# Three of five last-group projections of an SSD mixer moved into its step loop

## The chip, the cores and the metric

The kernel runs on one core of one Trainium2 chip. The metric is the device time of one execution in microseconds (us). The core has five engines with a queue each: TensorE (PE in the profile, its weight loads PEld), VectorE (DVE), ScalarE (ACT), GpSimd (POOL), and SyncE (SP), which here only issues DMAs. An engine works through its own queue in order; a waiting instruction holds up all that stand behind it on that engine.

## The reference, cut to what matters

Two layers of a streaming encoder take 640 tokens of width 1024: 512 of a new stream (four tiles of 128) and 8 x 16 of running streams (a fifth tile). Layer 0 is FFN, mixer, FFN; layer 1 is FFN, Mamba-2 mixer, FFN. Each is wrapped as `x = layer_norm(ALPHA * x + sublayer(x))`. The change is in the second mixer and what surrounds it:

```python
proj = x @ w_in                                   # z | x B C | dt
xbc  = silu(conv(xbc));  dt = softplus(dt_raw + dt_bias)
y, h_last = ssd_recurrence(xs, dt, a, bm, cm, h0)  # 4 groups of 8 heads, state 128
y  = y + d_skip * xs
yg = y * silu(z)                                  # per group of 512 channels
yg = yg * rsqrt(mean(yg ** 2) + RMS_EPS) * norm_g
out = yg @ w_out                                  # 2048 -> 1024
x = layer_norm(ALPHA * x + out)
```

All is in float32. The kernel splits each operand into a high and a low part that TensorE takes at full rate, and adds three products (`mm3`): high x high, low x high, high x low.

## The kernel before, in words

The mixer (`mixer1`) has four groups of heads and five token tiles, so 20 **steps** `(g, c)`, in the order of tiles `ORDER = (4, 0, 1, 2, 3)` in each group: first the tile of the running streams (4), then the new stream's four, whose state is handed on from tile to tile. Steps are counted from 0; steps 15 to 19 are the fourth group's, which the code calls `g == 3`. In the body of step i stand:

- `run_fill(1)`, twice in most steps: one input projection of a later group (`xbc`, `gate_in`) as filler for TensorE. There are 33; the last of them, the fourth group's last gate input, stands at the start of step 16, so steps 17 to 19 have none.
- `core_a` of the next step (loads of B, C, x rows and decays, L1688 to L1712; decay matrix, turned inputs, L1715 to L1739), mostly VectorE and ScalarE work.
- `core_b` of this step (L1747 to L1780: state product on TensorE, the state's decay on POOL at L1763, the sum at L1764, the outputs L1772 to L1779), or `core_s` for tile 4, which reads the running streams' states from tiles named `h0` (four of them, loaded before).
- `gate_out(g - 1, c)`: the out-projection of the group before, one step row later. It loads z rows from DRAM (L1824), multiplies (L1825), squares (L1826), adds up on POOL (L1828, L1829), sums over partitions by a matmul with ones (L1830), makes the RMS factor (L1832, L1833), splits the product into `og`, and runs 24 matmuls (`mm3`, L148) into two banks, which L1841 scales and adds to the residual `yacc`.

After the 20 steps the fourth group's five projections follow, tiles 0 to 4, each with its layer norm (`layer_norm`, L176 to L205: statistics L185 on VectorE, the power L188 on POOL, the scaling L192 on ScalarE, gamma and beta on VectorE L194 and POOL L195 to L197; for the last tile two whole-row VectorE operations, L199 and L205). A norm ends by putting its transposes (L220 to L222: into the channel-major `xhi`, `xlo` that the next matmuls read) on a list, `pend`; `run_pend` emits the oldest of the list. Gamma and beta are loaded by POOL's queue (L173) into `h0` places.

**Buffers.** Weights come by SP's queue into four `raw` tiles and are split (L101 and L102; with a row factor L127 and L128) into the pair tiles `w`, six in all, each of two units. `w1` is a single unit. A group's out-weights are four pair tiles. `ext` and `acc` are row tiles (two each) of the convolution and the gate inputs; `cst` holds the convolution's old rows, which only the `xbc` projections read. The z rows of the fourth group go into `ext` and `acc`, their split results into `og` or `csb`.

**The FFN after it** (`ffn`, ph `ffn3`) starts with two hidden blocks (f = 0, 1) on the first half of the tokens (tiles 0, 1) and then on the second (tiles 2 to 4), 48 matmuls each, with a `run_pend` after each.

**What sets the order.** The program text gives each instruction a rank and its dependences; a planner orders each engine's queue by these and its own estimates of durations, so that an instruction can come out ahead of others that stand before it in the text. `tc.issue_after(x)` keeps what it encloses behind x on x's engine.

## Time and profile before

| | |
|---|---|
| Median of 3 runs | 2508.24 us (2507.06 to 2510.02) |
| The profiled execution's own time | 2512.95 us |
| Its span, first to last instruction | 2511.2 us |
| Granted TensorE clock, mean | 0.999 |
| POOL busy | 382.3 us (15%) |
| DMA rate, mean | 130 GB/s |

How to read the views below: in a table of stretches (times from the span's start) each engine has its busy us and its number of instructions; the last three numbers are the granted clock, the mean busy share of the 16 DMA engines and GB/s. In a list of waits the engine, the tile and the line that waited stand first, then what it waited for, then total us, how often, and the longest. In a group of instructions: line, engine, operation, output and inputs with shapes, count, then busy us and mean ns of one, then the idle time before them. In a timeline: start, us, engine, line, operation, count, and in brackets the idle time before and what ended it.

### The profile page before, as it was taken

The page shows a single profiled execution, that of the slowest core. Times are in us where ns is not written, and L with a number is a line of the kernel's source. Part 1 is how long each engine was busy: PE and PEld are TensorE (multiplying, and loading weights), DVE is VectorE, ACT ScalarE, POOL GpSimd, SP SyncE. Part 2 cuts the span into 40 slices and gives each one's busy share as a digit, 9 for nine tenths or more (in the row PEclk, how much of TensorE's full clock was granted, in tenths as well). Part 3 has the DMA queues.
Part 4 walks back from the last instruction along what each step waited for, and adds up shares of the span by engine and source line. Part 5 has one row for each costly group of instructions (what it writes and reads, how often), then busy time and mean ns, then how long its engine had stood idle before and what let it go on. Part 6 is the DMA issues. An engine that isn't in the chain of part 4 may idle for free. (4 is left out here: it accounts for less than half of the span.)

```text
span 2511.2 us, 40776 instructions
## 1 busy us (share of the span) xinstructions
PE 2475.4 (99%) x15563; PEld 2277.1 (91%) x15563; DVE 2019.0 (80%) x3400; ACT 1285.9 (51%) x2415; POOL 382.3 (15%) x500
## 2 busy tenths in 40 slices
PE   9999999999999999999999999999999999999998
PEld 8999999978789999999999999999999879999897
DVE  7797787666878888878888887787686788898887
ACT  4444454336744555553455554567565543555542
POOL 0000001210130000013000002311111152211121
PEclk9999999999999999999999999999999999999999
DMA  5333344443222433461144434466565623555563
GB/s 187 110 99 99 120 145 138 145 152 114 91 84 68 122 94 106 110 167 58 59 121 111 117 101 133 152 197 189 161 213 149 203 72 102 160 146 168 155 172 113
DMA packets 179092, 326.63 MB, mean 130 GB/s; under 512 B 21408, under 2 KB 91040, under 8 KB 178384
## 3 DMA queue, kind: packets, MB, share of 16 engines
q1 hardware_dynamic: 164032, 293.83, 37.0%
q0 software_dynamic: 14864, 30.19, 6.2%
q8 instruction: 122, 2.00, 0.3%
q14 instruction: 74, 0.61, 0.1%
HBM read 259.56 MB, written 40.54 MB: 120 GB/s over the span
## 5 line engine op out<-in xcount | busy, mean ns | idle before, releaser
L101 ACT CAST w<-raw 128x512 fp32r<-128x512 f32 (+1 forms) x721 | 536.0, 773 | 333.5 <-DVE raw L368 150.9
L102 DVE TENSOR_TENSOR w<-raw,w 128x512 fp32r<-128x512 f32 (+2 forms) x721 | 626.6, 891 | 75.5 <-ACT w L101 73.2
L385 PE MATMUL bank<-xhi,w 128*128 128x320 f32 x2432 | 436.8, 309 | 2.7 <-DVE s L427 1.4
L385 PE MATMUL bank<-T,w 128*128 128x320 f32 x2736 | 430.6, 309 | 3.5 <-ACT bank L402 2.2
L385 PEld LDWEIGHTS bank<-T,w 128*128 128x128 f32 x2736 | 407.1, 188 | 7.3 <-ACT bank L402 5.2
L385 PEld LDWEIGHTS bank<-xhi,w 128*128 128x128 f32 x2432 | 377.2, 188 | 6.7 <-DVE s L427 2.2
L148 PE MATMUL bank<-xhi,w 128*128 128x256 f32 (+2 forms) x2272 | 360.0, 309 | 5.9 <-DVE yacc L1841 1.3
L148 PEld LDWEIGHTS bank<-xhi,w 128*128 128x128 f32 x2272 | 333.5, 187 | 16.1 <-ACT xhi L221 2.4
L148 PE MATMUL bank<-w,h 128*128 128x512 f32 (+1 forms) x1404 | 325.0, 389 | 0.6 <-ACT h L101 0.6
L148 PEld LDWEIGHTS bank<-w,h 128*128 128x128 f32 x1404 | 259.7, 188 | 53.6 <-ACT h L101 2.2
L385 PE MATMUL bank<-xlo,w 128*128 128x320 f32 x1216 | 228.2, 309 | 0.0
L368 DVE TENSOR_TENSOR raw<-raw 128x512 f32<-128x512 f32 x304 | 212.0, 697 | 3.4
L539 POOL DMA_DIRECT2D yacc<-ev x91 | 79.1, 902 | 746.8 <-ACT ev L538 659.6
L385 PEld LDWEIGHTS bank<-xlo,w 128*128 128x128 f32 x1216 | 190.9, 188 | 0.1
L148 PE MATMUL bank<-xlo,w 128*128 128x256 f32 (+2 forms) x1136 | 189.1, 307 | 0.0
L148 PEld LDWEIGHTS bank<-xlo,w 128*128 128x128 f32 x1136 | 170.2, 187 | 0.6
L526 PE MATMUL bank<-w,h 128*128 128x512 f32 x624 | 145.7, 389 | 0.0
L526 PEld LDWEIGHTS bank<-w,h 128*128 128x128 f32 x624 | 116.8, 188 | 24.7 <-DVE yacc L535 0.6
L535 DVE SCALAR_TENSOR_TENSOR yacc<-bank,yacc 128x512 f32<-128x512 f32 x91 | 62.6, 688 | 71.9 <-PE bank L526 71.9
L398 ACT COPY mx<-bank 128x320 f32<-128x320 f32 x152 | 64.5, 424 | 94.2 <-PE bank L385 93.2
L538 ACT ACTIVATE ev<-bank 128x512 f32<-128x512 f32 x91 | 54.1, 595 | 111.4 <-PE bank L526 94.3
L234 DVE SCALAR_TENSOR_TENSOR yacc<-bank,yacc 128x512 f32<-128x512 f32 x108 | 74.0, 687 | 44.8 <-PE bank L148 44.4
(442 smaller groups left out, 3434.5 us busy)
## 6 DMA issues: line engine op xcount, KB each, us to landing
raw<-in_w_gate_dram SPq DMA_DIRECT2D x88, 512.0 KB, 3.7
raw<-in_w_up_dram SPq DMA_DIRECT2D x88, 512.0 KB, 4.1
raw<-in_w_down_dram SPq DMA_DIRECT2D x88, 512.0 KB, 3.6
raw<-in_m_in_dram SPq DMA_DIRECT2D x52, 512.0 KB, 4.4
yacc<-ev POOLq DMA_DIRECT2D x91, 256.0 KB, 4.9
raw<-in_m_out_dram SPq DMA_DIRECT2D x24, 512.0 KB, 4.1
csb<-cs_d SPq DMA_DIRECT2D x20, 512.0 KB, 4.7
h<-in_ssd_h_dram SPq DMA_DIRECT2D x16, 512.0 KB, 6.3
```

Source lines behind the costliest of these rows:

```text
L101: nc.scalar.copy(hi, src)
L102: return nc.vector.tensor_tensor(lo, src, hi.bitcast(F32), op=ALU.subtract)
L148: state["pe"] = nc.tensor.matmul(ps, a, b, start=(k == 0), stop=(k == n - 1)).ins
L234: state["acc"] = nc.vector.scalar_tensor_tensor(ya, pb, scale, ya, op0=ALU.mult, op1=ALU.add).ins
L368: V.tensor_tensor(o, v, w, op=ALU.subtract)
L385: nc.tensor.matmul(ps, A[p][:, a, k * 128:k * 128 + 128], X[p][b][:, k, :], start=(first and n == 0), stop=(n == 11), skip_group_check=True)
L398: nc.scalar.copy(e[n], ps)
L526: nc.tensor.matmul(ps, a[:, u], b[:, v], start=(first and n == 0), stop=(n == 5), skip_group_check=True)
L535: V.scalar_tensor_tensor(ya, ps, 0.5 / ALPHA, ya, op0=ALU.mult, op1=ALU.add)
L538: nc.scalar.mul(e, ps, 0.5 / ALPHA)
L539: nc.gpsimd.dma_start(yacc[:, t, 512 * j:512 * j + 512], e, accum_op=ALU.add)
```

## The change

What it does:

- Three of the fourth group's five projections with their norms go into steps 17, 18 and 19: tile 4, then 0, then 1. The projection stands first in the step, the norm last; the steps get a `run_pend` after `core_b` or `core_s`. Tiles 2 and 3 follow the loop, each with its transposes list worked off between projection and norm. The tile whose norm is the last is now 3.
- The fourth group's out-weights are loaded in step 16: two before the last gate input, into the four `h0` places; two after it, into pair tiles.
- Gamma and beta are loaded in step 16 too, in half rows, into `ext` and `acc`.
- The z rows of the fourth group go into `cst`, and the split result into the single unit `w1`; for tile 3 into `zz` and `og`.
- In the FFN, the first `run_pend` is left out if only one tile is on the list.

```diff
-    def load_w(src, rows=None):
+    def load_w(src, rows=None, into=None):
         r = raw_tile()
         nc.sync.dma_start(r, src)
-        w = two_units()
+        if into is None:
+            w = two_units()
+            u = w[:, 0], w[:, 1]
+        else:
+            u = into
...
-    def layer_norm(t, g_bc, last):
+    def layer_norm(t, g_bc, last, end=NT - 1):
...
-        if t < NT - 1 and not last:
+        if t != end and not last:
...
+        elif isinstance(g_bc[0], list):
+            for c in (lo, hi):
+                nc.vector.scalar_tensor_tensor(y[:, c], y[:, c], mv[:, 0:1], gb(0, c), op0=ALU.subtract, op1=ALU.mult)
+            for c in (lo, hi):
+                state["ln"] = nc.vector.scalar_tensor_tensor(y[:, c], y[:, c], rs, gb(1, c),
+                                                             op0=ALU.mult, op1=ALU.add).ins
...
                     finish(f, o, L)
-                    run_pend()
+                    if h or f or len(pend) != 1:
+                        run_pend()
...
+            def load_wo(g, ks, into=lambda: None):
+                for k in ks:
+                    wo.setdefault(g, {})[k] = load_w(I["m1_out"][4 * g + k], chp[:, 1, 4 * g + k:4 * g + k + 1], into())
+
             def gate_out(g, c):
                 if g not in wo:
-                    wo[g] = [load_w(I["m1_out"][4 * g + k], chp[:, 1, 4 * g + k:4 * g + k + 1]) for k in range(4)]
+                    load_wo(g, range(4))
                 y = ys.pop((g, c))
-                if g == 3:
-                    zz = row_tile("acc" if c % 2 else "ext")[:, :512].rearrange("p (q t) -> p q t", t=128)
+                if g == 3 and c != 3:
+                    zz = cst.rearrange("p m b -> p (m b)")[:, :512].rearrange("p (q t) -> p q t", t=128)
                 else:
                     zz = wk.tile([128, 4, 128], F32, name="zz", bufs=1)
...
-                og = wk.tile([128, 4, 2, 128], F32R, name="csb" if g == 3 and c % 2 else "og", bufs=2 if g == 3 and c % 2 else 1)
-                split(og[:, :, 0], og[:, :, 1], y)
+                if g == 3 and c != 3:
+                    u = unit()
+                    og = [u[:, n].rearrange("p (q t) -> p q t", t=128) for n in range(2)]
+                else:
+                    u = wk.tile([128, 4, 2, 128], F32R, name="og", bufs=1)
+                    og = [u[:, :, n] for n in range(2)]
+                split(og[0], og[1], y)
...
+            norm = lambda c: layer_norm(c, g_bc, last, ORDER[-1])
             for i, (g, c) in enumerate(steps):
+                if i == 16:
+                    load_wo(3, (0, 1), lambda: [wk.tile([128, 2, 512], F32R, name="h0", bufs=4) for _ in range(2)])
+                if i >= 17:
+                    gate_out(3, steps[i - 2][1])
                 run_fill(1)
+                if i == 16:
+                    load_wo(3, (2, 3))
+                    g_bc = [[row_tile(n)[:, :512] for _ in range(2)] for n in ("ext", "acc")]
+                    load_gb(LN_OF[ph], g_bc)
                 if i + 1 < len(steps):
                     with tc.issue_after(state["pe"]) if i == 0 else ExitStack():
                         core_a(*steps[i + 1])
                 then = (core_b if c < 4 else core_s)(g, c)
+                run_pend()
                 run_fill(0 if i in (8, 14) else 1)
                 if then is not None:
                     then()
                 if g:
                     gate_out(g - 1, c)
+                if i >= 17:
+                    norm(steps[i - 2][1])
             share("azay", "b")
-            for c in range(NT):
+            for c in ORDER[-2:]:
                 gate_out(3, c)
-                if c == 0:
-                    g_bc = [wk.tile([128, 2, 512], F32, name="h0", bufs=4).rearrange("p a b -> p (a b)")
-                            for _ in range(2)]
-                    load_gb(LN_OF[ph], g_bc)
-                layer_norm(c, g_bc, last)
-                if c >= 2:
-                    run_pend()
+                run_pend()
+                norm(c)
```

## The prediction

> **What bounds the kernel now.** I read the page first, then a table of stretches around the end of the second mixer, the waits of TensorE's weight loader there, and the timeline between them.

> ```profile
> span 2511.2 us, 40776 instructions
> PE 2475.4 (99%) x15563; PEld 2277.1 (91%) x15563; DVE 2019.0 (80%) x3400; ACT 1285.9 (51%) x2415; POOL 382.3 (15%) x500
> ```

> TensorE carries the whole program and VectorE is second. A change at one place is worth only the TensorE time that is idle at that place, so the next view is local. The last gate input of the mixer ends on TensorE at about 1994; the step loop runs to about 2034.4; the five out-projections of the fourth group fill 2034.4 to 2067.7; the FFN's first half (tokens 0 to 255) runs until the second half starts at 2082.7.

> ```profile
> core 0: us, PE busy (x) PEld busy (x) DVE busy (x) ACT busy (x) POOL busy (x), PEclk, DMA share, GB/s
> 1969.20:1994.00 24.80, 24.80 (x168) 22.21 (x168) 16.18 (x30) 11.86 (x27) 6.08 (x7) 1.00 0.69 231
> ...
> 2002.80:2015.00 12.20, 10.07 (x61) 7.82 (x61) 12.20 (x22) 7.65 (x18) 5.16 (x6) 1.00 0.62 205
> ...
> 2025.80:2034.40 8.60, 8.60 (x54) 6.95 (x53) 6.68 (x14) 2.79 (x6) 3.63 (x6) 1.00 0.09 33
> 1994.00:2034.40 40.40, 37.05 (x226) 29.33 (x226) 36.29 (x67) 21.11 (x54) 15.58 (x20) 1.00 0.43 133
> 2034.40:2067.70 33.30, 32.47 (x156) 26.14 (x156) 26.98 (x54) 12.88 (x21) 22.93 (x22) 1.00 0.23 71
> 2067.70:2082.70 15.00, 13.50 (x115) 13.06 (x113) 13.34 (x22) 8.22 (x15) 8.43 (x6) 1.00 0.24 72
> ```

> Before 1994 TensorE is full and VectorE has a third of its time free. From 2002.8 to 2015.0 it is the reverse: VectorE works 12.20 of 12.20 us and TensorE waits. This is the step loop without its filler (the input projections have run out), and each step costs VectorE more than TensorE. From 2034.4 on TensorE is nearly full again. The granted clock is 1.00 throughout and DMA never above 0.69, so neither counts. What TensorE waits for between 1994 and 2082.7:

> ```profile
> PEld bank L148 <- DVE og L102: 1.8, 2, 1.6
> PEld bank L148 <- ACT og L101: 1.6, 1, 1.6
> PEld bank L148 <- DVE yacc L1841: 1.5, 1, 1.5
> PEld bank L1772 <- issue: 1.5, 4, 0.4
> PEld bank L1830 <- issue: 1.4, 4, 0.8
> PEld bank L148 <- ACT w L127: 1.2, 2, 1.0
> PEld bank L1719 <- DMA bx<-bcx_d: 0.6, 1, 0.6
> PEld bank L220 <- POOL yacc L196: 0.5, 2, 0.3
> ```

> The columns are total us, times, longest. All of it is 10.1 us of 88.7: that is the whole prize. The 1.5 at L1772 is 0.4 at every block of these 64-wide matmuls and stays. Of the 1.4 at L1830 the longest is 0.8 and the other three are 0.2 each, so 0.6 can go. Removable: 1.8 + 1.6 + 1.5 + 1.2 + 0.6 + 0.5 + 0.6 = 7.8 us.

> **The change part by part.** *Weights.* The out-weights of the fourth group are today caught behind those of the third, which hold four of the six pair tiles.

> ```profile
> 2036.13 2.73 DVE L128 SCALAR_TENSOR_TENSOR w<-raw,chp,w 128x512 fp32r<-128x512 f32 x4
> 2037.20 0.53 PEld L148 LDWEIGHTS bank<-w,csb 128*128 128x128 f32 x3 [1.04 <-ACT w L127]
> ```

> Two pair tiles are left for the first two of the four; the other two (four halves, 2.73 us on VectorE) come only at 2036, after the last third-group projection has let its tiles go, and TensorE waits 1.2 us for them. This, not the program order alone, is why no fourth-group projection can fill the idle of 2002 to 2020. With two weights in the places of the loaded states (free once step 15 has read them) and two in the pair tiles, all four can be there early in the stretch: the 1.2 goes, and 2.73 us of VectorE work moves to the stretch before 1994, which has 24.80 - 16.18 = 8.6 us free. The FFN's first four weights now find four free pair tiles at the end of the third group's projections, where today two are taken again by the out-weights.

> *Three tiles inside the steps.* What one tile brings along on each engine:

> ```profile
> L1841 DVE SCALAR_TENSOR_TENSOR yacc<-bank,rms,yacc 128x512 f32<-128x512 f32 x18 | 13.4, 745 | 2.5 <-POOL rms L1833 1.2 <-POOL ext L1828 0.7 <-PE bank L148 0.4
> L185 DVE BATCH_NORM_STATS2 st<-yacc 128x6 f32<-128x512 f32 x10 | 6.9, 688 | 0.1
> L222 DVE TENSOR_TENSOR xlo<-bank,xhi 128x512 fp32r<-128x512 f32 x8 | 5.2, 657 | 0.0
> L102 DVE TENSOR_TENSOR og<-yb,og 128x512 fp32r<-128x512 f32 x6 | 4.7, 779 | 0.4 <-ACT og L101 0.4
> L194 DVE TENSOR_TENSOR yacc<-yacc,h 128x512 f32<-128x512 f32 x4 | 3.5, 883 | 0.2 <-ACT yacc L192 0.2
> L1825 DVE TENSOR_TENSOR yb<-yb,zz 128x512 f32<-128x512 f32 x3 | 2.0, 679 | 0.0
> 2054.44 5.44 PEld L148 LDWEIGHTS bank<-w,csb 128*128 128x128 f32 x24
> 2053.35 0.90 PEld L220 LDWEIGHTS bank<-ident,yacc 128*128 128x128 f32 x8 [0.18 <-POOL yacc L196]
> ```

> VectorE: 2 x 0.745 + 0.679 + 0.779 for the projection, 2 x 0.688 + 0.883 for the norm, 2 x 0.657 for the turned copy: 6.5 us. TensorE: 5.44 + 0.90 = 6.3 us. (Some small ones are left out on both sides.) So a moved tile is neutral between the two: it doesn't relieve VectorE, it gives TensorE matmuls whose inputs are ready while VectorE works on the step. The fourth-group result of the tile is two steps old by then. Hence the waits for og, bx and the 0.6 at L1830 (4.6 us) have a 5.44 us block to lie under in each of steps 17, 18 and 19, and the 0.5 for POOL at the transposes has one too. In total VectorE has 36.29 + 26.98 + 13.34 = 76.6 us of work in the 88.7, 73.9 after the weights have left. TensorE needs 88.7 - 7.8 = 80.9. Both fit, but both are close to full in the same places, so not all 7.8 comes.

> What I take off is a wait that each norm brings along on VectorE (its waits in the same 88.7 us):

> ```profile
> DVE mv L191 <- POOL rs L188: 4.8, 3, 3.3
> ```

> In each norm VectorE stands until POOL has made the power, with everything behind it in its queue. Today this happens where TensorE is the bound and costs nothing; in the steps it costs. Bounds: nothing, where other VectorE work is put in between, and 3.3 a norm. The 3.3 is POOL still at the adds of the norm before it, as the timeline there shows; norms a whole step apart don't meet on POOL, so I take the mean of the two others, (4.8 - 3.3) / 2 = 0.75: 3 x 0.75 = 2.3 us.

> *The FFN's start.* Its second matmul group waits 1.5 us for a bank that the last projection's VectorE sum still holds. VectorE is as full there afterwards (the last tile's norm still stands there), so I count half as gone and take 0.7 off. The last tile's norm in four half rows instead of two whole ones adds a little to VectorE: by the 128x512 rows above, four of 0.69 to 0.75 are 2.8 to 3.0 us. Its transposes keep their place behind both first-half groups of the FFN, and those (the 15.0 us of the table) cover it; without that cover the second half would wait up to 3 us. The transposes of the tile before it do change place: they stood two projections after their own norm began, now one. Of that a rival below.

> *Loads.*

> ```profile
> zz<-z_d SPq DMA_DIRECT2D x15, 256.0 KB, 4.6
> 2005.09 1.02 DVE L1825 TENSOR_TENSOR yb<-yb,ext 128x512 f32<-128x512 f32 x1
> ```

> The z rows of four tiles now take turns in one buffer where today they have four (and so do their split results, in one unit tile), so each load waits on SP's queue for the previous tile's sum, and the next step's loads (B and C rows, decays) queue behind it. The sum it waits for is a step old when it comes up, so I cost it at nothing; without that cover it is one landing, 4.6 us, for one step. Four gamma and beta loads instead of two stand on POOL's queue, and there they wait until the last z row is stored, with the state product of the step behind them. That product has until VectorE adds to it, most of a step later, so nothing again; uncovered, it is one such transfer more.

> Sum: 7.8 - 2.3 - 0.7 = 4.8 us. The profiled execution took 2512.95 us, 1.75 over its span, and would take 2508.2; the median of the runs shown, 2508.24, is 4.7 below it, and by the same difference becomes 2503.4.

> **The rivals.** *All of it comes.* VectorE finds work in every wait for POOL and the bank wait goes too: 7.8 us, 2500.4. For it speaks VectorE's 12.1 us of idle in the 88.7 (76.6 busy); against it, that the idle isn't in 2002 to 2015, where TensorE needs it.

> *VectorE only gets longer.* If VectorE is the bound through all of steps 17 to 19, three tiles lengthen them by 3 x 6.5 and shorten the tail by 3 x 6.3. What remains is the weight wait, the POOL wait at the transposes and little else: 1.2 + 0.5 = 1.7 us, 2506.5. For it: 12.20 of 12.20. Against it: 6.68 us of work in the 8.6 before 2034.4 and the 2.73 that leave.

> *A wait in place of the one removed.* The transposes of the last tile but one stand ahead of the FFN's first matmuls in the program.

> ```profile
> 2057.63 0.68 DVE L185 BATCH_NORM_STATS2 st<-yacc 128x6 f32<-128x512 f32 x1
> ...
> 2066.69 1.03 PEld L220 LDWEIGHTS bank<-ident,yacc 128*128 128x128 f32 x8
> ```

> From this tile's second statistics to its transposes it is 9.1 us today, 10.6 with the two sums before (2 x 0.745), under two projections. Afterwards one projection and one tile's transposes cover 5.44 + 0.90 = 6.3 of it. If TensorE keeps the program's order, it stands 10.6 - 6.3 = 4.3 us, and 4.8 - 4.3 = 0.5 is left: 2507.7. Against it: the FFN's first half doesn't need this tile, and a planner that sees the wait puts those matmuls first.

> *The change does nothing.* The engines' order is made by a planner, not by the program text; if it kept the projections late, the time would be 2508.2. Against it: the row of 2005.09 is a fourth-group multiply that it has already pulled forward into step 17, so it does take work that is ready.

> *Slower: POOL's norm work beside a full VectorE.*

> ```profile
> L195 POOL TENSOR_TENSOR yacc<-yacc,h 128x512 f32<-128x512 f32 x4 | 6.7, 1677 | 5.6 <-ACT yacc L192 5.6
> L197 POOL TENSOR_TENSOR yacc<-yacc,h 128x512 f32<-128x512 f32 x4 | 6.1, 1535 | 0.3
> L196 POOL TENSOR_TENSOR yacc<-yacc,h 128x512 f32<-128x512 f32 x4 | 5.6, 1406 | 0.0
> ...
> 2062.57 1.46 DVE L194 TENSOR_TENSOR yacc<-yacc,h 128x512 f32<-128x512 f32 x1
> ```

> Each norm puts 1.68 + 1.54 + 1.41 = 4.6 us on POOL. Beside them a VectorE product of two SBUF tiles can take twice its time (1.46 at 2062.57, against 0.68 for the like product of L1825). In the tail this is free; in steps full of such products it is not. If VectorE lost all of POOL's time, three norms would cost 13.9 us: 13.9 - 4.8 = 9.1 slower, 2517.3. It decides from (4.8 + 5.0) / 3 = 3.3 us a norm. Against it: L194's mean is 0.883, so on average it lost little. [...]

> **How the numbers follow.** A measurement here tells 0.2%, 5.0 us, from no change. The forecast (3.0 to 6.5 us gained) gets 0.46, about half of it (0.24) beyond 5.0; all of it (over 6.5) 0.18; VectorE only longer 0.12; the transposes' wait 0.08; nothing 0.03; POOL 0.13. Faster: 0.24 + 0.18 = 0.42; same: 0.22 + 0.12 + 0.08 + 0.03 = 0.45; slower: 0.13. The range goes from 2 us below the full prize, 2498.4, taken as 2498, since the seven waits may have been counted short, to 2511: that takes in the three cases with little or no gain, with one missed landing on top of VectorE's (2506.5 + 4.6 = 2511.1), and leaves out the POOL case and a little below.

> **What would show it.** Right: the weight wait at L127 is gone; TensorE's waits for og fall under 1 us in all; the FFN's first matmuls start 3 to 6 us earlier counted from the last gate input; VectorE is over 0.93 busy from step 17 to the FFN. Wrong: new TensorE waits at L1830 or at L1753 for POOL, VectorE products in steps 17 to 19 at twice their time, a wait of some 4 us at the transposes before the FFN, or the first FFN weights being split after the last projection has ended. If the steps grow by more than the tail shrinks, the working fails at "neutral".

## The result, and the profile after

The changed kernel takes 2520.99 us, the kernel before 2508.01 us beside it (medians of 5 and 6 runs): a ratio of 1.0051, 95% interval 1.0041 to 1.0062, 13 us slower. A sixth run of the changed kernel, 3034.67 us at a mean TensorE clock of 0.752, is left out. The line numbers of the changed kernel are some ten to thirty higher: the split products are L152, the transposes L234, the norm L192 to L205, the core L1703 to L1794, the gate load L1843, its product L1844, GpSimd's two sums L1847 and L1848, the ones-product L1849, the yacc sums L1865. In the experiments they shift by a few lines more.

The page of the changed kernel's profiled execution (2519.91 us) shows the same matmuls and nearly the same busy times as before:

```profile
span 2518.2 us, 40795 instructions
...
PE 2478.1 (98%) x15563; PEld 2281.3 (91%) x15563; DVE 2021.8 (80%) x3402; ACT 1287.0 (51%) x2415; POOL 382.8 (15%) x502
```

So nothing that a page sums up has moved; the loss is local. I measure it on the prediction's stretch, from the end of the last gate input to the second half of the FFN's tokens, cut once at the FFN's first matmul. The table of stretches (us, then busy us and instructions of PE, PEld, DVE, ACT, POOL, then granted clock, DMA share, GB/s), first of the kernel before:

```profile
1994.01:2067.68 73.67, 69.49 (x380) 55.44 (x379) 63.27 (x121) 33.97 (x74) 38.49 (x41) 1.00 0.34 105
2067.68:2082.72 15.04, 13.52 (x115) 13.08 (x113) 13.36 (x23) 8.27 (x15) 8.45 (x6) 1.00 0.24 71
sum 88.71, PE 83.01 PEld 68.52 DVE 76.63 ACT 42.23 POOL 46.94; mean PE 41.50 PEld 34.26 DVE 38.32 ACT 21.12 POOL 23.47
```

and of the changed kernel:

```profile
1988.77:2069.95 81.18, 72.55 (x381) 58.84 (x380) 65.35 (x118) 35.48 (x75) 38.48 (x41) 0.94 0.27 86
2069.95:2090.73 20.78, 14.65 (x114) 14.16 (x112) 13.05 (x25) 5.50 (x9) 8.00 (x7) 0.92 0.27 83
sum 101.96, PE 87.20 PEld 73.00 DVE 78.40 ACT 40.98 POOL 46.48; mean PE 43.60 PEld 36.50 DVE 39.20 ACT 20.49 POOL 23.24
```

The stretch grew from 88.71 to 101.96, by 13.3 us: as much as the medians differ. (The two profiled executions differ by 7.0 us only: the one of before lies 4.9 over its median and reaches the end of the last gate input 5.2 us later, at 1994.01 against 1988.77.) Steps and tail give 7.5 of it, the FFN's first half 5.7. On TensorE, with the same matmuls, it is 4.2 us more of busy time (87.20 - 83.01), because the granted clock fell (from 1.00 to 0.94 and 0.92), and 9.1 us more of standing (14.76 against 5.70). VectorE works 1.8 us more and has 23.6 us free. No engine is full over the stretch; what grew is the waiting.

TensorE stood in three places. Its own rows in the timeline (start, duration, operation, count, idle time before it and what ended it):

```profile
2002.25 0.38 PE L1849 MATMUL bank<-ones,cst 128*128 128x2 f32 x2 [3.95 <-POOL cst L1848]
...
2003.18 1.05 PE L152 MATMUL bank<-w,w 128*128 128x512 f32 x2
...
2031.04 1.09 PE L234 MATMUL bank<-ident,yacc 128*128 128x128 f32 x4 [3.28 <-DVE bk L102]
...
2078.59 1.97 PE L234 MATMUL bank<-ident,yacc 128*128 128x128 f32 x8 [5.90 <-POOL yacc L204]
```

First, step 17 opens with tile 4's projection; its ones-product waits for a gate that has to go through memory (the last gate input ends at 1988.77), and the matmuls on step 18's core inputs `bx` queue behind it. Those inputs were late as well: their load goes out at 1995.85, 7.1 us behind the end of the last gate input (5.7 in the kernel before), and lands 5.6 us later, at 2001.45, 0.8 us before that product starts.

```profile
1995.85 0.32 SPq L1703 DMA_DIRECT2D bx<-bcx_d  x1
```

Second, tile 4's transposes in step 18 stand for a PSUM bank until VectorE has split `bk`. Third, tile 2's transposes stand inside the FFN's first products and wait for that tile's norm. Around each of the three, the clock (the same table of stretches, cut where the clock changes):

```profile
1999.44:2002.85 3.41, 0.60 (x4) 0.56 (x5) 2.43 (x6) 2.52 (x5) 2.31 (x3) 1.00 0.14 55
2002.85:2006.26 3.41, 3.41 (x10) 2.63 (x9) 1.00 (x2) 0.00 (x0) 1.39 (x3) 0.50 0.28 82
2026.74:2030.15 3.41, 1.02 (x16) 0.78 (x16) 3.41 (x7) 2.90 (x11) 1.94 (x3) 1.00 0.00 0
2030.15:2033.57 3.42, 2.53 (x10) 2.35 (x11) 3.42 (x7) 1.48 (x4) 0.80 (x1) 0.50 0.00 0
2033.57:2036.98 3.41, 3.41 (x10) 2.74 (x9) 3.30 (x10) 0.46 (x1) 0.94 (x2) 0.50 0.17 36
2074.53:2077.94 3.41, 0.00 (x0) 0.00 (x0) 3.34 (x6) 0.00 (x0) 3.33 (x3) 1.00 0.83 269
2077.94:2081.36 3.42, 2.77 (x13) 2.77 (x14) 1.98 (x3) 1.33 (x3) 2.56 (x3) 0.50 0.00 0
```

A 3.41 us window in which TensorE worked 0.60, 1.02 and 0.00 us is followed by one or two such windows at exactly half clock, in which a pair of 128x512 products takes 1.05 us; from 2006.45 on the same pair takes 0.62 to 0.64. Half of the 12.1 us worked at 0.50 (3.41 + 2.53 + 3.41 + 2.77) is 6.1 us lost. (Busy time shows only 4.2 of it as a difference; where the other 1.9 us went, no view shows.)

### The profile page after: what moved, and what is told of

It is laid out like the page before. It is cut to its first block, busy times and chain, and to the rows that moved or that the text cites. A ratio compares the mean times of both kernels' runs of the same rounds, so it can differ in the third digit from the quotient of the medians.

```text
span 2518.2 us, 40795 instructions
## 1 busy us (share of the span) xinstructions
PE 2478.1 (98%) x15563; PEld 2281.3 (91%) x15563; DVE 2021.8 (80%) x3402; ACT 1287.0 (51%) x2415; POOL 382.8 (15%) x502
## 4 chain that ended last, share of the span: by engine, by line
PE 85%; DVE 9%; issue 2%; DMA 2%; ACT 2%; POOL 1%; SPq 0%; POOLq 0%; DVEq 0%; ACTq 0%
PE bank L152 34%; PE bank L400 32%; PE bank L541 10%; PE bank L1084 3%; DVE w L102 1%; DVE raw L383 1%; PE bank L234 1%; PE bank L920 1%; PE bank L1787 1%; DVE h L102 0%; DMA csb<-cs_d 0%; PE bank L1337 0%; DVE yacc L248 0%; PE bank L1773 0%; DVE st L192 0%
## 5 line engine op out<-in xcount | busy, mean ns | idle before, releaser
L101 ACT CAST w<-raw 128x512 fp32r<-128x512 f32 (+1 forms) x721 | 536.0, 773 | 332.0 <-DVE raw L383 148.9
L102 DVE TENSOR_TENSOR w<-raw,w 128x512 fp32r<-128x512 f32 (+2 forms) x721 | 626.6, 891 | 76.6 <-ACT w L101 74.3
L152 PE MATMUL bank<-xhi,w 128*128 128x256 f32 (+2 forms) x2272 | 358.8, 309 | 3.4 <-DVE hf L323 1.3
L152 PEld LDWEIGHTS bank<-xhi,w 128*128 128x128 f32 x2272 | 333.2, 187 | 13.0 <-ACT xhi L235 2.4
L152 PE MATMUL bank<-w,h 128*128 128x512 f32 (+1 forms) x1404 | 325.2, 389 | 0.0
L152 PEld LDWEIGHTS bank<-w,h 128*128 128x128 f32 x1404 | 259.7, 188 | 53.1 <-ACT h L101 1.6
L152 PE MATMUL bank<-xlo,w 128*128 128x256 f32 (+2 forms) x1136 | 189.6, 307 | 0.0
L152 PEld LDWEIGHTS bank<-xlo,w 128*128 128x128 f32 x1136 | 170.5, 187 | 0.7
L248 DVE SCALAR_TENSOR_TENSOR yacc<-bank,yacc 128x512 f32<-128x512 f32 x108 | 73.9, 686 | 44.5 <-PE bank L152 44.0
## 6 DMA issues: line engine op xcount, KB each, us to landing
yacc<-ev POOLq DMA_DIRECT2D x91, 256.0 KB, 4.8
```

What stands on the lines that cost most here:

```text
L101: nc.scalar.copy(hi, src)
L102: return nc.vector.tensor_tensor(lo, src, hi.bitcast(F32), op=ALU.subtract)
L152: state["pe"] = nc.tensor.matmul(ps, a, b, start=(k == 0), stop=(k == n - 1)).ins
L248: state["acc"] = nc.vector.scalar_tensor_tensor(ya, pb, scale, ya, op0=ALU.mult, op1=ALU.add).ins
```

## The experiments

Theory A: the loss is these long rests, made by TensorE's fixed order, and the half clock behind each. Theory B: VectorE is the bound of the steps, and a rest taken away comes back at the next instruction. Theory C: it is the shared buffers and the early loads. Each time is a median; ratios are to the kernel before on the same chip, with their 95% intervals. The experiments ran on four chips, on which the kernel before took 2508.4 to 2509.6 us, so a difference of 1 us between runs of two chips says nothing. Each trace is that of one execution. Where stretches are compared, it is the stretch above.

**Tile 2's transposes later.** In the tail, `run_pend()` only for tile 2, so that its transposes come behind the FFN's first block:

```
                 gate_out(3, c)
-                run_pend()
+                if c == 2:
+                    run_pend()
                 norm(c)
```

> The changed kernel, but the transposes of the last tile but one (tile 2) come after the FFN's first block instead of inside its first matmul group. Theory A (the loss is three long TensorE waits, each with a stretch at half the granted clock behind it: 4.4 us at the ones-matmul of step 17, 3.5 us at tile 4's transposes in step 18, 6.1 us at tile 2's transposes): the 6.1 us wait and the slow clock behind it (0.79 and 0.86 over 10 us, so about 1.2 us) go, 7 us faster than the changed kernel, about 2514.5. Theory B (VectorE is the bound and a wait that is taken away comes back at the next place): under 2 us faster, about 2520.

2517.37 us, 1.0033 (1.0021 to 1.0046): 4 us under the change, the stretch 4.3 shorter, between A's 7 and B's 2. TensorE's weight loads show what is left of the wait of 6.10 (5.90 in PE's own row):

```profile
2080.16 0.86 PEld L234 LDWEIGHTS bank<-ident,yacc 128*128 128x128 f32 x8 [2.85 <-POOL yacc L204]
```

This wait is real, and about a third of the loss.

**The moved projection behind the core.** `gate_out(3, ...)` stands just ahead of `gate_out(g - 1, c)` instead of at the head of the step:

> The changed kernel, but the fourth-group projection of steps 17 to 19 stands behind core_a and core_b of the step, not ahead of them. Theory A: the ones-matmul no longer stands in front of work that is ready, so its 4.4 us wait and the 4 us at 0.59 of the clock behind it (1.7 us lost) go, about 6 us faster than the changed kernel, 2515.5; the waits at the transposes stay. Theory B: the same VectorE work is in the steps, so under 2 us faster, about 2520.

2522.55 us, 1.0053 (1.0040 to 1.0065): no gain. Theory A's number missed. The ones-product no longer waits in step 17, but a rest of 2.6 us on PE stands there still, now at step 18's core inputs (L1734 below), with one window of half clock behind it. The load of those inputs (out at 1998.47, 5.2 us) and the ScalarE square that the row names both end at 2003.7. The transposes wait more (weight loader's waits in the stretch: total, times, longest):

```profile
PEld bank L234 <- POOL yacc L204: 11.4, 4, 6.5
PEld bank L1734 <- ACT zz L1845: 2.8, 1, 2.8
```

**The rests filled.** 12 products of 128x512 without use ahead of step 17's ones-product, 10 ahead of tile 4's transposes; the outputs stay as they are:

> The changed kernel with 12 matmuls of 128x512 whose result nobody reads put into the wait of step 17 and 10 into that of step 18 (0.23 us each, 2.7 and 2.3 us); no wait is taken away and nothing is left out. Theory A with the clock: the idle pieces get too short for the clock to fall, the granted clock stays at 1.00 behind them, and the 1.7 us and 3 us lost there come back: 4 to 5 us faster than the changed kernel, about 2517. If the slow matmuls behind the waits have another cause than idle time, or the clock falls by total idleness: no change or a little slower, 2521 to 2523.

2519.13 us, 1.0039 (1.0025 to 1.0053): 1.9 us under the change in the median, with intervals that overlap, where A expected 4 to 5. The clock is 1.00 through steps 17 to 19, but the transposes behind them wait longer in all (7.7 against 6.7), with three windows of half clock from 2061 on:

```profile
PEld bank L234 <- POOL yacc L204: 7.7, 2, 4.9
```

By itself this tells A from B no further.

**The buffers alone.** Early weights and half-row gamma and beta as in the change, gate and split results by turns in the new places (tiles 1 and 3) and in `zz` and `og`, but all five projections behind the loop:

> Only the buffers and loads of the change, none of the moves: the fourth group's out-weights are loaded in step 16 into the loaded states' places and two pair tiles, gamma and beta early in half rows, z rows and split results in turn in two buffers each; all five projections and norms stand behind the loop as in the kernel before. Theory A (the moves make the loss): the weight wait of 1.2 us is gone and nothing else changes, 1 to 2 us faster than the kernel before, about 2506.5. Theory C (the buffers are at fault: one-buffer turns or the weights' places): slower than the kernel before by several us, 2512 to 2520.

2515.33 us, 1.0023 (1.0013 to 1.0033): 6.6 us slower than before, where A expected a gain of 1 to 2. So there is a loss in which no projection is moved, half as large as that of the change. TensorE stands at the core's inputs, for the load of `bx`, in steps 17 and 18:

```profile
2004.88 0.46 PE L1734 MATMUL bank<-bx 128*128 128x128 f32 x2 [2.88 <-DMA bx<-bcx_d]
...
2017.45 0.77 PE L1734 MATMUL bank<-bx 128*128 128x128 f32 x2 [3.30 <-DMA bx<-bcx_d]
```

**All transposes later.** The first edit, and `run_pend()` at the end of steps 17 to 19 instead of in their middle:

> The edit: in steps 17 to 19 the pending transposes come at the end of the step, behind the third group's projection, in place of before it; and tile 2's transposes come behind the FFN's first block (as in the run with the last transposes later). Nothing else moves. Theory A (the loss is the long rests of TensorE in its written order, each with a stretch of half clock behind it): the 3.5 us wait at tile 4's transposes in step 18 and the granted clock of 0.50 behind it go (about 6 us), and the 4.2 us of the last transposes again: 2521.6 - 10 = 2511 to 2513 us; step 17's wait of about 4 us at the ones-product stays with its clock. Theory B (VectorE is the bound of these steps, so that a wait taken away at one instruction comes back at the next): no more than the 4.2 us of the last transposes, 2516 to 2518 us, with a new wait of 3 us or more elsewhere in steps 18 and 19.

2517.58 us, 1.0033 (1.0021 to 1.0046): as B had it, nothing beyond the first edit. Step 17's rest is there as before, and the weight loader's 3.49 us ahead of tile 4's transposes in step 18 (3.28 in PE's row) came back at the ones-product that stands there instead, for the same split of `bk`:

```profile
2004.73 0.50 PEld L1849 LDWEIGHTS bank<-ones,cst 128*128 128x128 f32 x2 [4.37 <-POOL cst L1848]
...
2034.50 0.50 PEld L1849 LDWEIGHTS bank<-ones,zz 128*128 128x128 f32 x2 [3.49 <-issue]
```

So the second rest was not the transposes' doing. Whose, the next run shows.

**And step 17's rest filled.** On the run before, the 12 products ahead of step 17's ones-product again, nothing in step 18:

```
+                if i == 17:
+                    warm(12)
                 if i >= 17:
                     gate_out(3, steps[i - 2][1])
```

> The run with the transposes behind the steps, and 12 products of 128x512 whose result is thrown away in front of step 17's ones-product, where TensorE waits some 4 us. They leave the outputs as they are. They can take no wait away; they can only keep the granted clock up behind it. Theory A: the clock stays at 1.00 behind step 17's wait, which is worth the 1.9 us that the products at half clock cost there: 2 us under the run without them. Theory B: nothing, within 1 us, since VectorE goes at its own pace.

2509.81 us, 1.0005 (0.9996 to 1.0013): 7.8 us less, by work that nobody needs. A expected 2 and B under 1. The sums of the two stretches, without the filling:

```profile
1991.25:2091.43 100.18, 88.66 (x493) 74.12 (x492) 77.32 (x142) 40.75 (x84) 45.70 (x47) 0.91 0.28 86
```

and with it:

```profile
1988.94:2080.74 91.80, 85.73 (x505) 72.22 (x503) 77.96 (x142) 40.47 (x84) 46.19 (x47) 0.98 0.31 94
```

TensorE is busy 2.9 us less although it does 12 products more, and stands 5.5 us less (6.07 against 11.52). Its other matmuls stand in nearly the same order through steps 17 and 18. Step 18's rest fell to 1.23:

```profile
2027.19 0.30 PEld L1849 LDWEIGHTS bank<-ones,zz 128*128 128x128 f32 x2 [1.23 <-issue]
```

So most of that rest was the echo of step 17's. The likely way, which no run shows by itself: at half clock (0.50 from 2003.53 to 2010.36 in the run without the filling) TensorE hands its projections late to VectorE, VectorE's sums and norm come late, and a step further on TensorE waits for VectorE. VectorE has the same work in both runs (77.3 and 78.0 us), so its amount of work, theory B, did not make these 7.8 us.

**The gate ahead of the projection.** Instead of filling, on the run with all transposes later: the gate's load, product, square and GpSimd's sums stay at the head of the step, the ones-product, the split and the projection go behind the core:

```
                 if i >= 17:
-                    gate_out(3, steps[i - 2][1])
+                    gate_front(3, steps[i - 2][1])
...
+                if i >= 17:
+                    gate_out(3, steps[i - 2][1])
                 if g:
                     gate_out(g - 1, c)
```

> The run with the transposes behind the steps, and the moved tile's product with the gate, its square and GpSimd's sums at the head of the step as in the change, but its ones-product, its split and its projection behind the step's core work, so that the core work covers the round trip of the gate through memory. Theory A: step 17's wait of about 4 us and its half clock go, 5 to 6 us under the run without this edit: 2505 to 2508 us, below the kernel before. Theory B: VectorE sets the pace, the wait comes back at the core work or at the projections, and the time is within 2 us of the run without this edit.

2509.58 us, 1.0003 (0.9994 to 1.0012): 8.0 us less than without it, somewhat more than A's 5 to 6. With the edits of the runs before it, the changed kernel's 13 us are gone by order alone:

```profile
1988.37:2077.43 89.06, 81.69 (x493) 68.15 (x492) 78.88 (x142) 39.88 (x84) 46.11 (x47) 1.00 0.31 96
```

Now the longest rest is at step 18's core inputs, for `bx`, which lands as late as in the change (5.6 us behind its issue at 1995.46):

```profile
2001.19 0.46 PE L1734 MATMUL bank<-bx 128*128 128x128 f32 x2 [2.96 <-DMA bx<-bcx_d]
```

So step 17's rest was shortened by a quarter and moved, not taken away. The trace has no half clock behind it, by where the rest lies on the clock's grid (last section). That is one execution of 2506.15 us; the eleven runs go from 2505.75 to 2513.57, and whether the others had a drop is not known.

**The weights alone.** The kernel before with `load_wo(3, ...)` as in the change; gamma and beta in the two `xe` tiles after the last step:

> The kernel before, with one part of the change: the fourth group's out-weights are loaded and split in step 16, two of them into the places of the loaded states; no projection is moved. The scale and shift of the norm go into the two tiles of the core's split inputs behind the last step, in place of the loaded states. Theory A: the 1.2 us that the projections wait for weights go and nothing else moves: 1 to 1.5 us faster than the kernel before. Theory C (what is loaded and split early costs the steps as much or more, by VectorE's four splits beside steps that are full, or by transfers ahead of the steps' own): 1 to 5 us slower than the kernel before, with longer waits in steps 17 to 19.

2512.80 us, 1.0014 (1.0005 to 1.0023): 3.7 us slower, C's side. The rests:

```profile
PEld bank L1723 <- DMA bx<-bcx_d: 3.5, 1, 3.5
PEld bank L1723 <- ACT csb L1721: 2.0, 1, 2.0
```

The suspect stands in VectorE's order: the last weight's two splits ahead of step 17's core work.

```profile
1992.40 1.42 DVE L132 SCALAR_TENSOR_TENSOR w<-raw,chp,w 128x512 fp32r<-128x512 f32 x2
1993.73 1.22 DVE L1727 TENSOR_TENSOR csb<-csb,cbm 128x1024 f32<-128x1024 f32 x1
```

**The weights alone, the last one later.** The same, with only that weight loaded in step 18:

```
                 if i == 16:
-                    load_wo(3, (2, 3))
+                    load_wo(3, (2,))
+                if i == 18:
+                    load_wo(3, (3,))
```

> The run with the weights alone (no projection moved), and the last of the four out-weights loaded two steps later, as in the kernel before. If the 3.7 us that the weights alone cost come from the last weight's splits standing ahead of step 17's core work (step 18's core inputs late, TensorE resting for 1.8 and 3.1 us, half clock behind each), they go: 2507 to 2509 us, within 1 us of the kernel before or up to 1.2 faster. If they come from the two weights in the places of the loaded states, or from the norm's scale and shift in another place, 2512 to 2513 as before.

2507.88 us, 0.9993 (0.9984 to 1.0002): 5 us less, and no longer slower than before; the forecast gain of 1.2 lies in the interval, and so does nothing. The stretch is the shortest of all:

```profile
1989.29:2077.29 88.00, 82.64 (x493) 68.31 (x493) 74.92 (x140) 39.62 (x84) 45.85 (x48) 1.00 0.34 106
```

So 1.4 us of VectorE work in the wrong place cost 5 us; the weight's load and its two ScalarE halves moved along with it. The clock is part of these 5 us: with the weight early the trace has two windows of 3.41 us at a clock of 0.50 (from 2002.84 and from 2016.49, 1.7 us lost in each), with it late none (1.00 in the row above). It probably explains the run with the buffers alone as well, which waits at the same inputs; that was not tried by itself. The change has the same two splits in the same place (at 1990.26), ahead of its late `bx`.

**On from the gate run: three edits.** The last FFN's transposes one product group later (tile 2's behind the gate products of its second block, tile 3's behind the up products); the last weight later, in step 17 here; both.

> The run with the gate ahead of the projection, and in the last FFN's first half tile 2's transposes one group of products later (behind the gate products of its second block) and tile 3's behind the up products, so that the norm of tile 2 has another 3 us. Theory A (each rest of TensorE in its written order counts): the 2.5 us wait at tile 2's transposes goes, 2 to 2.5 us under the run without this edit, 2507 to 2508 us. Rival (the second half of the tokens then waits for the last tile's copies in its place): within 1 us.

2507.90 us, 0.9990 (0.9982 to 0.9999): 1.7 us less, with intervals that just overlap.

> The run with the gate ahead of the projection, and the last of the four out-weights loaded and split one step later, behind step 17's gate product, so that its two VectorE splits (1.4 us) do not stand ahead of step 17's core work. Theory A: the load of step 18's core inputs, which waits for VectorE's last reads of step 16's, goes out 1.4 us earlier and ahead of the FFN's 512 KB of weights; TensorE's 3.0 us rest for it shrinks to under 1.5 us: 1.5 to 2.5 us under the run without this edit, 2507 to 2508 us. Rival (the splits cost VectorE the same wherever they stand): within 1 us.

2512.62 us, 1.0011 (1.0002 to 1.0020): 3 us more, with intervals that overlap, where a gain of 1.5 to 2.5 was expected: a miss. The rest for `bx` did shrink, from 2.96 to 1.3, but the planner had another order to make, and a rest of 2.6 opened at a ones-product for GpSimd, with a window of half clock behind it:

```profile
PEld bank L1857 <- POOL zz L1849: 2.6, 1, 2.6
...
PEld bank L1734 <- DMA bx<-bcx_d: 1.3, 1, 1.3
```

> Both edits together on the run with the gate ahead of the projection. Theory A: the two gains add up, 4 us under that run: 2504 to 2506 us, faster than the kernel before by 3 to 5 us and than the changed kernel by 16. Rival: the time of that run, 2509 us, within 1.5.

2509.61 us, 0.9996 (0.9988 to 1.0005): no sum of gains.

**What the moved tiles gain at all.** On the run with the FFN's transposes later, in two ways: a gate tile for each moved tile; the moved norms on VectorE instead of ScalarE and GpSimd.

> The run with the FFN's transposes later, and the gate of each moved tile loaded into a tile of its own (one of the six that hold the core's outputs) in place of one shared one, so that a gate's load need not wait for the ones-product of the tile before. Theory A (what still holds the moved tiles is the shared buffer): VectorE's and TensorE's waits at the gate product and the ones-product (1.2 us twice) shrink, 1 to 2.5 us under the run without this edit. Theory D (VectorE, stretched by GpSimd's norm, sets the pace): within 1 us.

2508.52 us, 0.9999 (0.9990 to 1.0008): the shared gate buffer costs nothing that can be measured.

> The run with the FFN's transposes later, and the three moved tiles' norms written as four products on VectorE (subtract and scale, scale and shift, by halves) in place of one pass on ScalarE, one product on VectorE and three on GpSimd. GpSimd keeps only the power. Per tile VectorE does some 3.0 us in place of the 1.7 to 1.9 that its one product took beside GpSimd, and its other products beside the norm go back from 1.1 to 1.9 to 0.7 us (some 1.5 us per tile). Theory D (GpSimd's norm beside VectorE is what eats the gain): 1 to 3 us under the run without this edit. Theory A or a VectorE that is merely full: 0 to 3 us over it.

2508.60 us, 0.9999 (0.9990 to 1.0008): neither gained nor lost. In the stretch GpSimd worked 34.40 us there; with its norm it worked 46.48 in the change:

```profile
1990.61:2080.43 89.82, 84.52 (x493) 71.19 (x492) 80.08 (x148) 36.98 (x81) 34.40 (x38) 0.96 0.31 95
```

The last four runs moved only two tiles, or one, into later steps, with the last weight loaded in step 18; first with each tail tile's transposes behind the next projection:

> The run with the FFN's transposes later, with only tiles 4 and 0 moved, into steps 18 and 19 in place of 17 and 18, and the last out-weight loaded in step 18 as in the kernel before. Step 17 then has no gate product that waits for the gate's round trip, and no rest of 3 us at step 18's inputs. If that first moved tile is what ate the gain: 2504 to 2506 us. If each moved tile costs as much as it brings: 2507.5 to 2509, like the weights alone.

> The same with only tile 4 moved, into step 19. If each moved tile brings something once its rests are gone: between the weights alone (2508) and the run with two tiles, 2506 to 2507. If each costs what it brings: the weights alone, 2508, within 1 us.

2520.05 us (1.0042, 1.0028 to 1.0056) and 2516.70 us (1.0032, 1.0019 to 1.0044). All of the expectation missed, since new rests came up behind the loop. With one tile it is a set of transposes ahead of its norm's end:

```profile
2062.08 1.14 PEld L234 LDWEIGHTS bank<-ident,yacc 128*128 128x128 f32 x6 [6.95 <-POOL yacc L204]
```

Then with the distance that the kernel before has (two norms ahead of each tile's transposes):

> The run with two tiles, and in the tail each tile's transposes behind the next but one projection and its norm, as in the kernel before. The waits of 6.4 and 3.8 us at transposes and ones-product behind the loop and the half clock behind them (1.7 to 3 us) go: about 12 us off 2520, 2507 to 2509. If the moved tiles gain once the first of them stands clear of the gate's round trip: 2504 to 2506. If they cost what they bring: 2507.5 to 2509, like the weights alone.

> The same edit on the run with one tile: the waits of 7.0 and 1.2 us at transposes and the two windows of half clock go, some 10 us off 2516.7: 2506 to 2508. If one moved tile gains: at least 1 us under the weights alone (ratio to the kernel before under 0.9989); if it costs what it brings, the same as the weights alone (ratio 0.999 to 1.000).

2519.63 us (1.0044, 1.0030 to 1.0058) and 2518.34 us (1.0043, 1.0030 to 1.0055). With two tiles the ones-product of tile 1 waited 6.39 us, since GpSimd had tile 0's norm ahead of that tile's second sum. GpSimd's timeline there:

```profile
2045.83 1.78 POOL L203 TENSOR_TENSOR yacc<-yacc,ext 128x512 f32<-128x512 f32 x1 [1.55 <-ACT yacc L201]
2047.57 1.17 POOL L1850 TENSOR_TENSOR zz<-zz 128x256 f32<-128x256 f32 x1
2048.70 1.26 POOL L204 TENSOR_TENSOR yacc<-yacc,acc 128x512 f32<-128x512 f32 x1
2049.93 1.26 POOL L205 TENSOR_TENSOR yacc<-yacc,acc 128x512 f32<-128x512 f32 x1
2051.15 0.45 POOL L1851 TENSOR_TENSOR zz<-zz 128x128 f32<-128x128 f32 x1
```

With one tile the transposes just ahead of the FFN waited:

```profile
2073.02 0.29 PEld L234 LDWEIGHTS bank<-ident,yacc 128*128 128x128 f32 x2 [6.25 <-POOL yacc L204]
```

These four say again what one badly placed instruction costs, and nothing on what a moved tile is worth. That stays open. What can be said: three moved tiles with better order (2507.90, ratio 0.9990) and no moved tile with the weights early (2507.88, ratio 0.9993) are the same time, though the first still has the last weight's splits in their bad place and a rest of 2.92 us. The first of them is the best version of the change that was found, 13.1 us under the change and 0.1% under the kernel before, with an interval that ends just short of no change.

## Why the prediction was wrong

Forecast were 4.8 us gained, measured 13 us lost.

**The prize was counted too large.** The prediction took the weight loader's 10.1 us of waits as TensorE's idle time and 7.8 of them as removable. But the loader works ahead of the array (its loads for L1758 start at 2014.91, the products at 2015.14), and in those 88.71 us the array itself stood 5.70 us (88.71 - 83.01). The row below ends the wait for `og` that the loader shows as 1.56:

```profile
2011.30 4.00 PE L148 MATMUL bank<-w,og 128*128 128x512 f32 x16 [1.12 <-DVE og L102]
```

By these figures, with all idle time gone the gain could not have passed 5.7 us, and the 4.8 forecast would have needed most of it.

**The new work was weighed, but not placed.** The step that failed on the path is "gives TensorE matmuls whose inputs are ready". For tile 4 they are not: its core result is two steps old, but its gate comes from the last gate input, through memory, and from the end of that input to the ones-product it is 13.5 us (1988.77 to 2002.25). Placed at the head of step 17, that product and its 24 matmuls hold the core's matmuls of step 18 until 2009.72, though their inputs landed at 2001.45. For the first 3 us of the 3.95 us rest those inputs were not there either; what the order adds is the last 0.8 us and the products at half clock ahead of the core. Two of the prediction's signs of being wrong came true, a TensorE wait at the ones-product for POOL and one of over 4 us at the transposes before the FFN; VectorE, to be over 0.93 busy up to the FFN, was 0.80 busy (65.35 of 81.18). The engine totals that the prediction compared were about right: VectorE 78.4 us in the stretch against 76.6, no engine over-full, "neutral" not refuted. Where a queue is worked in order, as those 0.8 us show of TensorE's, such totals say nothing on who stands behind whom. The profile of before could not show this wait, but the gate's store, load, product, square and two sums could have been added up from its rows; the row of 2005.09 that the prediction shows, a fourth-group multiply, stands 11.1 us behind the end of the last gate input.

**"The granted clock is 1.00 throughout … so neither counts".** It was true of before, whose longest rest in the stretch was 1.29 us, and was carried over to a kernel with rests of 3.28 to 5.90. Half clock cost 4.2 us by the busy times, and through its echo in step 18 more: the filling run got 7.8 us by keeping the clock up over one rest (0.98 in the stretch in place of 0.91). How much such a filling brings hangs on what stands behind it: in the changed kernel itself two of them brought 1.9.

**The rival of the transposes was right in mechanism and too small in chance and size.** Forecast 4.3 us at tile 2's transposes with a chance of 0.08; measured 5.9 on PE, with half clock behind it. The size failed at the start of the chain. VectorE's timeline in the changed kernel:

```profile
2063.84 0.75 DVE L1865 SCALAR_TENSOR_TENSOR yacc<-bank,rms,yacc 128x512 f32<-128x512 f32 x1 [1.66 <-POOL rms L1852]
2064.51 0.68 DVE L102 TENSOR_TENSOR w<-raw,w 128x512 fp32r<-128x512 f32 x1
...
2068.77 0.68 DVE L192 BATCH_NORM_STATS2 st<-yacc 128x6 f32<-128x512 f32 x1
```

Tile 2's first sum waits 1.7 us for a power that GpSimd makes behind the norm of tile 1, and from there to the second statistics lie 4.9 us with three of the FFN's weight splits between; to the transposes it is 14.8 us from the first sum, where the forecast had 10.6. "A planner that sees the wait puts those matmuls first" held in part: 20 of the first FFN group's 24 products stand ahead of the transposes, 2.5 us.

**Weights and loads, costed at nothing.** The wait at L127 and the waits for `og` went, as forecast. But the early weights were not free: as the change places them, without any moved tile, they cost 3.7 us where 1.2 was to be gained, through 1.4 us of VectorE work ahead of step 17's core, which sends step 18's inputs out late, and the half clock behind the rests that follow. The cover that was named (8.6 us free before 1994) is there, but the last weight's splits come behind it. Put right, the forecast of 1.2 stands within the error. The z rows that take turns in one buffer do make VectorE wait 2.4 us in step 18 of the changed kernel, within the named bound of one landing; tiles of their own gained nothing.

**The norm.** VectorE's wait for the power, forecast 2.3, was 1.3 for three. The slower rival (GpSimd's norm beside a full VectorE) had the sign and nearly the size, 2517.3, by a mechanism that the runs do not bear out: on the well-ordered run, norms without GpSimd's passes took the same time (2508.60 against 2507.90 us). That VectorE loses all of GpSimd's time, which its 13.9 us assume, no run shows: in the stretch of the changed kernel VectorE's product in the norm (L202) took 1.28 us in the mean, 1.48 at 2020.69, where the like product at 2026.24 (L1844) took 0.68, and VectorE's busy time in all grew by 1.8 us. What GpSimd's norm does cost is its place in GpSimd's own queue, ahead of the next tile's sum (6.39 us at a ones-product in the run with two tiles and far transposes).

By the prediction's own test ("the FFN's first matmuls start 3 to 6 us earlier counted from the last gate input") it is refuted at once: they start 7.5 us later (81.18 against 73.67).

## What to carry to other kernels

Work moved into a gap must be checked instruction by instruction against what its inputs wait for and who queues behind it: 13 us were lost and won back here with nearly the same work on each engine. Count the prize on the engine that does the work, not on the loader ahead of it (5.70 us against 10.1 here). And when a change can make TensorE rest for about 2 us or more, add the half clock behind that rest (here 29 windows with 2.02 us or more of standing, each with one at 0.50 behind it), and look one step further on for its echo (3.49 us with step 17's half clock, 1.23 without).

## What the runs showed of the hardware

```profile
1996.40:1999.81 3.41, 1.84 (x20) 1.18 (x18) 3.28 (x5) 2.53 (x3) 0.00 (x0) 1.00 0.95 355
1999.81:2003.22 3.41, 2.03 (x17) 2.02 (x18) 1.42 (x3) 2.24 (x9) 2.85 (x4) 1.00 0.54 162
```

A like rest of 2.92 us in the run with the FFN's transposes later did have it (its grid):

```profile
1999.23:2002.64 3.41, 1.27 (x11) 1.30 (x12) 1.38 (x4) 2.33 (x6) 2.22 (x4) 1.00 0.63 199
2002.64:2006.05 3.41, 3.41 (x14) 2.93 (x12) 2.82 (x5) 2.72 (x11) 0.77 (x2) 0.50 0.03 9
```

And in the run with the weights alone a window with nearly half of it worked was followed by half clock:

```profile
1999.43:2002.84 3.41, 1.66 (x21) 1.20 (x20) 3.33 (x5) 2.48 (x3) 0.00 (x0) 1.00 0.94 347
2002.84:2006.26 3.42, 3.42 (x17) 3.32 (x16) 2.71 (x4) 3.42 (x14) 3.11 (x3) 0.50 0.69 241
```

So a window need not be idle as a whole to have half clock behind it: here 1.75 us of standing (3.41 - 1.66) were enough, in another run 1.94 us were not (from 2073.07, the last weight later on the gate run), and 2.0 us or more always were.

The rate of the split products, in the kernel before at a granted clock of 1.00:

```profile
2026.07 1.05 PE L1753 MATMUL bank<-bx,hst 128*128 128x128 f32 x8
2026.88 0.94 PE L1758 MATMUL bank<-xe,bk 128*128 128x512 f32 x3
...
2029.02 5.84 PE L148 MATMUL bank<-w,og 128*128 128x512 f32 x24
2034.69 0.28 PE L1830 MATMUL bank<-ones,ext 128*128 128x2 f32 x2
```

The 24 split products of 512 columns are 5.67 us from start to next start, 0.24 each; the four float32 products of 128 columns at L1753 (eight records) 0.81 us, 0.20 each.
